# PEER routing of a two-layer trunk: one comparison and one product per eight tokens for the one-hot tiles, and sub-key scores issued in turns

## The chip, the cores and the metric

The kernel runs on one core of one Trainium2 chip. The metric is the device time of one execution in microseconds; each kernel is run several times and the median counts. The engines have short names in the profile: PE is the matrix engine (PEld its weight loads), DVE the vector engine, ACT the scalar engine, POOL the general-purpose engine, SP the engine whose queue issues most of the transfers.

## The reference

The reference is one inference step of a two-layer trunk over 128 context tokens and 512 latent tokens of width 1024. Each layer is a token mixer followed by a PEER expert mixer. Both are normalised and modulated; only the expert mixer matters here:

```python
q = (xc @ wq).reshape(P_BLOCK, P_HEADS, 2, P_DKEY // 2)
s = jnp.einsum('chpd,hpkd->chpk', q, sub_keys)
sv, si = lax.top_k(s, P_TOPK)                       # 16 of 128 per head and half
cand = sv[:, :, 0, :, None] + sv[:, :, 1, None, :]  # 16 x 16 candidates
fs, fi = lax.top_k(cand, P_TOPK)                    # 16 experts per head
eidx = jnp.take_along_axis(cidx, fi, axis=-1)       # cidx = i * 128 + j
g = jax.nn.softmax(fs, axis=-1)
act = jax.nn.gelu(jnp.einsum('cd,chkd->chk', xc, u[eidx]))
return jnp.einsum('chk,chkd->cd', g * act, v[eidx])
```

There are 8 heads, two halves of 64 numbers each, 128 sub-keys per half and 16384 experts, each named by a pair (i, j).

## The kernel before

The program runs mixer 0, PEER 0, mixer 1, PEER 1. A PEER layer has two phases.

In the routing phase (502 to 985 us in layer 0, the same again about 2005 us later in layer 1) the tokens come in five tiles of 128: tile 0 is the context, tiles 1 to 4 are latent. `scores` multiplies each tile's queries with the sub-keys: sixteen products of 64 rows, eight on the lower 64 rows of PE (row tile 0) and eight on the upper (row tile 1), in groups of four into one PSUM buffer, which ACT copies to SBUF. There are two such buffers (tag `sp`), shared with the transposes of `to_hk`. `topk` does the two-stage selection on DVE: sixteen rounds over the sub-keys, eight rounds (one for each head, five operations each) over the candidates `cand`, then the softmax weights `g` (the difference on DVE, Exp on ACT, the sum `gs` on DVE), and one-hot selections `eq` of 2048 elements that give the expert's `i` and `j` (tile `ij`).

For latent tokens the kernel does not gather experts. It computes all products S = u . h with PE (one S tile is 128 experts by 512 tokens, 24 matmuls: `h2h` and `h2l` are the tokens in two parts, `uh` and `ul` the expert rows in two parts, `uh` cast by ACT and `ul` made by DVE at L220; `ge` is the Gelu of S on ACT) and a matrix G of the weights, 128 by 128 per token. 72 of the 128 S tiles are computed in the routing phase, between its steps (`S_ahead`). G of a token is the product of two one-hot matrices. `to_hk` transposes i, j and g on PE, ACT copies them to `iT`, `jT` and, via `g32`, DVE makes the two halves `gh` and `gl` of g. For each group of eight tokens `build` makes on DVE the one-hot tile `oj` of j, the one-hot tile `oi` of i, and its products with `gh` and `gl` (both called `o`), 1024 half-precision elements per partition each. `place` multiplies on PE, sixteen small matmuls per group into two PSUM buffers called `G` (four in rotation), which ACT copies out into `stg`. Sixteen groups belong to a tile; those of tile tt are built and placed while the top-k of the next tile runs, and the last sixteen in a tail after tile 4. Groups 0 to 63 count through a layer.

The program is written in the order of the loops, but the framework's list scheduler decides the order of instructions on each engine in the routing phase. Each engine then works through its row strictly in order. The phase that follows, in which the expert outputs are computed, keeps the written order.

Of the kernel before, what the change touches and what calls it, by code (L numbers as in the profile page):

```python
# [13 lines left out]
F32 = mybir.dt.float32  # L14
F32R = mybir.dt.float32r
F16 = mybir.dt.float16
# [4 lines left out]
OP = mybir.AluOpType  # L21
# [4 lines left out]
P = 128  # L26
# [3 lines left out]
TS = 512  # L30
# [22 lines left out]
def _trunk(ctx, tc, nc, I, O, n_phases):  # L53
# [12 lines left out]
    ident = const("ident", [P, P])  # L66
# [1049 lines left out]
    def peer(l, last_layer):  # L1116
        with ExitStack() as s:
# [45 lines left out]
            with ExitStack() as s2:  # L1163
                qp = s2.enter_context(tc.tile_pool(reuse_waits="tile", name=f"pq{l}", bufs=1))
                sub = qp.tile([P, 8, P], F32, name=f"sub{l}")
                nc.sync.dma_start(sub, I["subT"][l])
                qT = qp.tile([P, 8, T], F32, name=f"qT{l}")
                with ExitStack() as s3:
                    wp = s3.enter_context(tc.tile_pool(reuse_waits="tile", name=f"pw{l}", bufs=2))
                    tp = s3.enter_context(tc.tile_pool(reuse_waits="tile", name=f"pt{l}", bufs=2))  # L1170
# [24 lines left out]
                    for n in range(NC):  # L1195
                        wh, wl, raw = ws.pop(n) if n in ws else wload(wp, I["pwq"][l, n], P, "w")
                        ps = ppn.tile([P, 2, 512], F32, name=f"pqs{l}_{n}", tag="b2")
                        for c in range(NC):
                            for k, (a, b) in enumerate(((wh, h2h), (wl, h2h), (wh, h2l))):
                                nc.tensor.matmul(ps[:, 0, :], a[:, c], b[:, c], start=(c == 0 and k == 0),  # L1200
                                                 stop=(c == NC - 1 and k == 2))
                        for c in range(NC):
                            nc.tensor.matmul(ps[:, 1, :TP], raw[:, c], ph32[:, c], start=(c == 0),
                                             stop=(c == NC - 1))
# [3 lines left out]
                    for x in range(2):  # L1208
                        ps = ppn.tile([P, 2, 512], F32, name=f"phT{l}_{x}", tag="b2")
# [4 lines left out]
                cp = s2.enter_context(tc.tile_pool(reuse_waits="tile", name=f"pc{l}", bufs=1))  # L1214
                tp = s2.enter_context(tc.tile_pool(reuse_waits="tile", name=f"pk{l}", bufs=2))
                ohp = s2.enter_context(tc.tile_pool(reuse_waits="tile", name=f"poh{l}", bufs=2))
                pk = s2.enter_context(tc.tile_pool(reuse_waits="tile", name=f"ppk{l}", bufs=2, space=PSUM))
                iota16 = cp.tile([P, 16, 8], F16, name=f"iota16{l}")
                nc.sync.dma_start(iota16, I["iota"])
                iota2 = cp.tile([P, P, 2], F16, name=f"iota2{l}")  # L1220
                nc.sync.dma_start(iota2, I["iota2"])
                iT = cp.tile([P, TS], F16, name=f"iT{l}")
                jT = cp.tile([P, TS], F16, name=f"jT{l}")
                gh = cp.tile([P, TS], F16, name=f"gh{l}")
                gl = cp.tile([P, TS], F16, name=f"gl{l}")

                def scores(tt):
                    nm = f"{l}_{tt}"
                    sc_ = tp.tile([P, 16, P], F32, name=f"sc{nm}", tag="sc", bufs=1)
                    for q4 in range(4):  # L1230
                        p, h0 = q4 % 2, (q4 // 2) * 4
                        rr = slice(p * 64, (p + 1) * 64)
                        ps = pk.tile([P, 4, P], F32, name=f"scp{nm}_{q4}", tag="sp")
                        for r in range(4):
                            nc.tensor.matmul(ps[:, r], qT[rr, h0 + r, tt * P:(tt + 1) * P], sub[rr, h0 + r],
                                             start=True, stop=True)
                        nc.scalar.copy(sc_[:, h0 * 2 + p:h0 * 2 + 8:2], ps)
                    return sc_

                def topk(tt, sc_, step):  # L1240
                    nm = f"{l}_{tt}"
                    sv = tp.tile([P, 16, 16], F32, name=f"sv{nm}", tag="sv")
                    si = tp.tile([P, 16, 16], U32, name=f"si{nm}", tag="si")
                    for r in range(16):
# [7 lines left out]
                    sif = tp.tile([P, 2, 16, 8], F16, name=f"sif{nm}", tag="sif")  # L1252
                    nc.vector.tensor_copy(sif.rearrange("p q a h -> p h q a"),
                                          si.rearrange("p (h q) a -> p h q a", q=2))
                    cand = tp.tile([P, 8, 112], F32, name=f"cand{nm}", tag="cand", bufs=1)
                    svh = sv.rearrange("p (h q) a -> p h q a", q=2)
                    nc.vector.tensor_tensor(
                        cand[:, :, 0:64].rearrange("p h (a b) -> p h a b", b=16),
# [20 lines left out]
                    gs = tp.tile([P, 8], F32, name=f"gs{nm}", tag="gs")  # L1279
# [20 lines left out]
                    def hk(t):  # L1300
# [3 lines left out]
                                            op=OP.subtract)  # L1304

                    ij = tp.tile([P, 2, P], F32, name=f"ij{nm}", tag="ij", bufs=1)
                    for q in range(2):
                        step(25 + 3 * q)
                        eq = tp.tile([P, 16, 16, 8], F16, name=f"eq{nm}_{q}", tag="eq", bufs=1)
                        nc.vector.tensor_tensor(eq, abk[:, q].unsqueeze(1).to_broadcast([P, 16, 16, 8]),  # L1310
                                                iota16.unsqueeze(2).to_broadcast([P, 16, 16, 8]),
                                                op=OP.is_equal)
                        nc.vector.tensor_tensor(eq, eq, sif[:, q].unsqueeze(2).to_broadcast([P, 16, 16, 8]),
                                                op=OP.mult)
                        for w in (8, 4, 2):
                            nc.vector.tensor_tensor(eq[:, :w], eq[:, :w], eq[:, w:2 * w], op=OP.add)
                        nc.vector.tensor_tensor(ij[:, q].rearrange("p (k h) -> p k h", h=8), eq[:, 0], eq[:, 1],
                                                op=OP.add)
# [1 line left out]
                    return gk, ij  # L1320

                def to_hk(tt, g, ij):
                    ts = slice((tt - 1) * P, tt * P)
                    ps = pk.tile([P, 4, P], F32, name=f"hk{l}_{tt}", tag="sp")
                    nc.tensor.transpose(ps[:, 0], ij[:, 0], ident)
                    nc.tensor.transpose(ps[:, 1], ij[:, 1], ident)
                    nc.tensor.transpose(ps[:, 2], g, ident)
                    nc.scalar.copy(iT[:, ts], ps[:, 0])
                    nc.scalar.copy(jT[:, ts], ps[:, 1])
                    g32 = tp.tile([P, P], F32, name=f"g32{l}_{tt}", tag="g32")  # L1330
                    nc.scalar.activation(g32, ps[:, 2], AF.Copy, scale=GSC)
                    nc.vector.tensor_copy(gh[:, ts], g32)
                    nc.vector.tensor_tensor(gl[:, ts], g32, gh[:, ts], op=OP.subtract)

                stg = [None]

                def build(grp):

                    ts = slice(grp * 8, (grp + 1) * 8)

                    def bc(t):
                        return (t[:, ts].rearrange("p (b t) -> p b t", t=2).unsqueeze(2)
                                .to_broadcast([P, 4, P, 2]))
                    io = iota2.unsqueeze(1).to_broadcast([P, 4, P, 2])
                    oj = ohp.tile([P, 4, P, 2], F16, name=f"oj{l}_{grp}", tag="oj")
                    oi = ohp.tile([P, 4, P, 2], F16, name=f"oi{l}_{grp}", tag="oi", bufs=1)
                    o1 = ohp.tile([P, 4, P, 2], F16, name=f"o1{l}_{grp}", tag="o1")
                    o2 = ohp.tile([P, 4, P, 2], F16, name=f"o2{l}_{grp}", tag="o2")
                    nc.vector.tensor_tensor(oj, bc(jT), io, op=OP.is_equal)  # L1349
                    nc.vector.tensor_tensor(oi, bc(iT), io, op=OP.is_equal)  # L1350
                    nc.vector.tensor_tensor(o1, oi, bc(gh), op=OP.mult)
                    nc.vector.tensor_tensor(o2, oi, bc(gl), op=OP.mult)
                    return oj, o1, o2

                def place(grp, oj, o1, o2):
                    if grp % 4 == 0:
                        stg[0] = ohp.tile([P, P, 32], F32, name=f"stg{l}_{grp}", tag="stg")
                    for q in range(2):
                        ps = pk.tile([P, 4, P], F32, name=f"G{l}_{grp}_{q}", tag="G", bufs=4)
                        for r in range(4):  # L1360
                            t = q * 4 + r
                            b, h = t // 2, t % 2
                            nc.tensor.matmul(ps[:, r], oj[:, b, :, h], o1[:, b, :, h], start=True, stop=False)
                            nc.tensor.matmul(ps[:, r], oj[:, b, :, h], o2[:, b, :, h], start=False, stop=True)  # L1364
                        t0 = (grp % 4) * 8 + q * 4
                        nc.scalar.activation(stg[0][:, :, t0:t0 + 4].rearrange("p i t -> p t i"), ps,  # L1366
                                             AF.Copy, scale=1.0 / GSC)
                    if grp % 4 == 3:
                        for a, b in ((0, NI),) if grp < 63 else ((0, 8), (8, NI)):
                            nc.sync.dma_start(Gd[grp // 4, :, a:b], stg[0][:, a:b])  # L1370
# [18 lines left out]
                for tt in range(NT):  # L1389
# [6 lines left out]
                    sc_ = scores(tt)  # L1396
# [3 lines left out]
                    g, ij = topk(tt, sc_, step)  # L1400
# [21 lines left out]
            with ExitStack() as s2:  # L1422
# [156 lines left out]
                with tc.manual_schedule():  # L1579
# [5 lines left out]
                    for y in range(NMAIN[0], CH, 2):  # L1585
                        r = rp.tile([P, 2, TS], F32, name=f"gr{l}_{y}", tag="row")
# [5 lines left out]
                    for cc in range(NB):  # L1592
                        nm = NMAIN[cc]
                        todo = None
                        ges = {}
                        for x in range(nm):
                            i = cc * CH + x
                            ps = S_mm(i, us.pop(i))
# [55 lines left out]
                        for dt in range(NC):  # L1654
                            n = cc * NC + dt
                            ps = out_mm(n, order)
# [151 lines left out]
```

## Time and profile before

| | us |
|---|---|
| Median of 3 runs | 4017.03 (4014.59 to 4021.36) |
| Profiled execution | 4011.71 |
| Its span in the trace | 4009.9 |
| PE busy | 3900.3 (97%) |
| DVE busy | 2955.4 (74%) |
| ACT busy | 1554.4 (39%) |
| POOL busy | 726.7 (18%) |

The profiled execution was 5.3 us below the median of the runs; outside its span lie 1.8 us. Times below count from the span's start. A row of a timeline gives start, duration, engine, line, operation, written tile `<-` read tiles and, in brackets, the idle time ahead of the instruction and what ended it. An engine starts an operation before the one ahead has wholly ended, so the step from start to start is shorter than the duration when nothing is waited for.

### The profile page before, as it was taken

To read this page: it belongs to the slowest core of one execution; us is meant where nothing else is said; L and a number is where in the kernel's file an instruction comes from. 1 tells how busy PE (TensorE), PEld (TensorE's weight loads), DVE (VectorE), ACT (ScalarE), POOL (GpSimd) and SP (SyncE) were. 2 spreads that over 40 slices of the span, in tenths; PEclk is the share of its full clock that TensorE was granted. 3 is DMA by queue.
4 is the path that set the end of the run, shared out by engine and by line. 5 is a ranking of instruction groups with operands and counts; after the bars stand their busy time and mean duration, and the time that the engine had idled before them with its cause. 6 is when DMAs were issued, how large, how long until landed. Compare 5 with 4: busy or idle time off the path is not lost.

```text
span 4009.9 us, 57042 instructions
## 1 busy us (share of the span) xinstructions
PE 3900.3 (97%) x21578; PEld 3242.2 (81%) x21578; DVE 2955.4 (74%) x6091; ACT 1554.4 (39%) x2320; POOL 726.7 (18%) x687
## 2 busy tenths in 40 slices
PE   7989999999999999999999999999999999999998
PEld 5958887888888888888889778888887888888887
DVE  5265389996778778787775663899967777777875
ACT  3344235566332322323343552355663323223231
POOL 0000000000334333243100110000003343333432
PEclk9989999999999999999999999999999999999999
DMA  5144134556888888888552012345568888888884
GB/s 181 55 169 143 54 126 179 200 195 248 295 278 296 294 283 305 272 294 299 193 183 87 17 38 70 127 178 201 195 248 296 280 295 293 285 303 272 297 301 166
DMA packets 363929, 850.80 MB, mean 212 GB/s; under 512 B 27858, under 2 KB 172164, under 8 KB 356868
## 3 DMA queue, kind: packets, MB, share of 16 engines
q1 hardware_dynamic: 289012, 576.04, 41.3%
q0 software_dynamic: 74640, 271.10, 19.5%
q8 instruction: 170, 2.79, 0.3%
q14 instruction: 107, 0.88, 0.1%
HBM read 738.12 MB, written 108.92 MB: 211 GB/s over the span
## 4 chain that ended last, share of the span: by engine, by line
PE 70%; DVE 13%; issue 8%; DMA 4%; ACT 3%; POOL 2%; SPq 0%; POOLq 0%; DVEq 0%; ACTq 0%
PE O L1528 9%; PE O L1532 9%; PE O L1529 9%; PE S L1141 8%; PE S L1142 7%; PE S L1144 7%; PE ow L246 4%; PE pqs L1200 2%; PE et L246 2%; DVE ul L220 2%; PE ef L435 1%; PE ewops L335 1%; PE owops L335 1%; POOL gu L1435 1%; PE CS L979 1%
## 5 line engine op out<-in xcount | busy, mean ns | idle before, releaser
L1141 PE MATMUL S<-h2h,uh 128*128 128x512 f32 x2048 | 811.8, 397 | 9.7 <-ACT ge L1149 5.5
L1528 PE MATMUL O<-Wh,vh 128*128 128x512 f32 x2048 | 798.3, 390 | 7.4 <-ACT Wh L1491 5.0
L1142 PE MATMUL S<-h2l,uh 128*128 128x512 f32 x2048 | 799.6, 391 | 0.0
L1529 PE MATMUL O<-Wh,vl 128*128 128x512 f32 x2048 | 797.3, 389 | 0.0
L1532 PE MATMUL O<-Wl,vh 128*128 128x512 f32 x2048 | 781.7, 389 | 0.0
L1144 PE MATMUL S<-h2h,ul 128*128 128x512 f32 x2048 | 589.4, 389 | 0.0
L219 ACT CAST vh<-v_raw 128x1024 fp32r<-128x1024 f32 x256 | 269.7, 1053 | 804.4 <-PE O L1532 754.4
L1435 POOL DMA_INDIRECT gv<-in_pv_dram,eidx x256 | 356.5, 1393 | 795.2 <-DVE acc L1451 771.1
L1141 PEld LDWEIGHTS S<-h2h,uh 128*128 128x128 f32 x2048 | 385.6, 188 | 94.9 <-ACT uh L219 7.8
L1528 PEld LDWEIGHTS O<-Wh,vh 128*128 128x128 f32 x2048 | 384.7, 188 | 90.2 <-ACT Wh L1491 7.2
L1532 PEld LDWEIGHTS O<-Wl,vh 128*128 128x128 f32 x2048 | 384.8, 188 | 80.4
L1144 PEld LDWEIGHTS S<-h2h,ul 128*128 128x128 f32 x2048 | 384.4, 188 | 80.0
L220 DVE TENSOR_TENSOR ul<-u_raw,uh 128x1024 fp32r<-128x1024 f32 x256 | 312.2, 1220 | 185.7 <-ACT uh L219 141.1
L1529 PEld LDWEIGHTS O<-Wh,vl 128*128 128x128 f32 x2048 | 384.8, 188 | 79.3
L1142 PEld LDWEIGHTS S<-h2l,uh 128*128 128x128 f32 x2048 | 386.0, 188 | 76.9
L1435 POOL DMA_INDIRECT gu<-in_pu_dram,eidx x256 | 321.5, 1256 | 520.3 <-DVE dots L1442 369.3
L219 ACT CAST uh<-u_raw 128x1024 fp32r<-128x1024 f32 x256 | 269.1, 1051 | 338.3 <-PE S L1142 312.4
L220 DVE TENSOR_TENSOR vl<-v_raw,vh 128x1024 fp32r<-128x1024 f32 x256 | 312.4, 1220 | 113.3 <-ACT vh L219 110.1
L1451 DVE SCALAR_TENSOR_TENSOR acc<-gv,dots,acc 128x1024 f32<-128x1024 f32 x256 | 327.7, 1280 | 44.8 <-DMA gv<-in_pv_dram,eidx 42.5
L1442 DVE CUSTOM_DVE_ANT_0 gu<-gu,h2p 128x1024 f32<-128x1024 f32 x256 | 311.3, 1219 | 48.4 <-DMA gu<-in_pu_dram,eidx 47.0
L1366 ACT ACTIVATE stg<-G 128x512 f32<-128x512 f32 x256 | 261.0, 1161 | 0.7 <-PE G L1364 0.7
L1429 POOL MEMSET acc<- 128x1024 f32 x2 | 1.9, 958 | 1338.9 <-DVE oj L1349 760.1
(402 smaller groups left out, 5909.4 us busy)
## 6 DMA issues: line engine op xcount, KB each, us to landing
u_raw<-in_uT_dram SPq DMA_DIRECT2D x256, 512.0 KB
v_raw<-in_vR_dram SPq DMA_DIRECT2D x256, 512.0 KB
gt<-Gd SPq DMA_DIRECT2D x64, 1024.0 KB
Gd<-stg SPq DMA_DIRECT2D x30, 2048.0 KB
adaw<-in_adaw_dram SPq DMA_DIRECT2D x80, 512.0 KB
Sd<-ge SPq DMA_DIRECT2D x144, 256.0 KB
gr<-Sd SPq DMA_DIRECT2D x134, 256.0 KB
w_raw<-in_ow_dram SPq DMA_DIRECT2D x12, 1024.0 KB
```

The lines of the kernel that those rows point to most:

```text
L219: nc.scalar.copy(hi, raw)
L220: nc.vector.tensor_tensor(lo, raw, hi.bitcast(F32), op=OP.subtract)
L1141: nc.tensor.matmul(ps, hi[:, c], h2h[:, c], start=(c == 0), stop=False)
L1142: nc.tensor.matmul(ps, hi[:, c], h2l[:, c], start=False, stop=False)
L1144: nc.tensor.matmul(ps, lo[:, c - 5], h2h[:, c - 5], start=False, stop=(c == NC + 5 - 1))
L1366: nc.scalar.activation(stg[0][:, :, t0:t0 + 4].rearrange("p i t -> p t i"), ps, AF.Copy, scale=1.0 / GSC)
L1435: nc.gpsimd.indirect_dma_start(out=r[:], out_offset=None, in_=I[table], in_offset=bass.IndirectOffsetOnAxis(ap=eidx2[:, k:k + 1], axis=0))
L1442: nc.vector.tensor_tensor_reduce(r, r, h2p, 1.0, 0.0, OP.mult, OP.add, dots[:, k:k + 1])
L1451: nc.vector.scalar_tensor_tensor(acc, r, dots[:, k:k + 1], acc, op0=OP.mult, op1=OP.add)
L1528: nc.tensor.matmul(ps, hi[:, order[y]], Wh, start=(y == 0), stop=False)
L1529: nc.tensor.matmul(ps, lo[:, order[y]], Wh, start=False, stop=False)
L1532: nc.tensor.matmul(ps, hi[:, x], Ws[n // NC * CH + x][1], start=False, stop=(y == CH + lag - 1))
```

## The change

`iT` and `jT` become one tile `jiT`, `gh` and `gl` one tile `ghl`, each laid out by groups of eight tokens. `build` makes both one-hot tiles with one comparison of 2048 elements (`oo`) and both gated tiles with one product of 2048 elements (`og`), in which the one-hot half of i is read twice. `oo` and `og` have two buffers each; before, `oj` and the two `o` had two and `oi` one. `cand` shares a buffer with `eq`. In `scores` two PSUM buffers are opened at once and the matmuls are written in turns on the two row tiles, the copies behind them.

```diff
-                    for q4 in range(4):
-                        p, h0 = q4 % 2, (q4 // 2) * 4
-                        rr = slice(p * 64, (p + 1) * 64)
-                        ps = pk.tile([P, 4, P], F32, name=f"scp{nm}_{q4}", tag="sp")
+                    for h0 in (0, 4):
+                        pss = [pk.tile([P, 4, P], F32, name=f"scp{nm}_{h0}_{p}", tag="sp") for p in range(2)]
+
                         for r in range(4):
-                            nc.tensor.matmul(ps[:, r], qT[rr, h0 + r, tt * P:(tt + 1) * P], sub[rr, h0 + r],
-                                             start=True, stop=True)
-                        nc.scalar.copy(sc_[:, h0 * 2 + p:h0 * 2 + 8:2], ps)
+                            for p, ps in enumerate(pss):
+                                rr = slice(p * 64, (p + 1) * 64)
+                                nc.tensor.matmul(ps[:, r], qT[rr, h0 + r, tt * P:(tt + 1) * P], sub[rr, h0 + r],
+                                                 start=True, stop=True)
+                        for p, ps in enumerate(pss):
+                            nc.scalar.copy(sc_[:, h0 * 2 + p:h0 * 2 + 8:2], ps)
...
-                    cand = tp.tile([P, 8, 112], F32, name=f"cand{nm}", tag="cand", bufs=1)
+                    cand = tp.tile([P, 8, 112], F32, name=f"cand{nm}", tag="eq", bufs=1)
...
-                    nc.scalar.copy(iT[:, ts], ps[:, 0])
-                    nc.scalar.copy(jT[:, ts], ps[:, 1])
+                    for q in range(2):
+                        nc.scalar.copy(jiT[:, gs, q], by8(ps[:, q]))
...
-                    io = iota2.unsqueeze(1).to_broadcast([P, 4, P, 2])
-                    oj = ohp.tile([P, 4, P, 2], F16, name=f"oj{l}_{grp}", tag="oj")
-                    oi = ohp.tile([P, 4, P, 2], F16, name=f"oi{l}_{grp}", tag="oi", bufs=1)
-                    o1 = ohp.tile([P, 4, P, 2], F16, name=f"o1{l}_{grp}", tag="o1")
-                    o2 = ohp.tile([P, 4, P, 2], F16, name=f"o2{l}_{grp}", tag="o2")
-                    nc.vector.tensor_tensor(oj, bc(jT), io, op=OP.is_equal)
-                    nc.vector.tensor_tensor(oi, bc(iT), io, op=OP.is_equal)
-                    nc.vector.tensor_tensor(o1, oi, bc(gh), op=OP.mult)
-                    nc.vector.tensor_tensor(o2, oi, bc(gl), op=OP.mult)
-                    return oj, o1, o2
+                    oo = ohp.tile([P, 8, P, 2], F16, name=f"oo{l}_{grp}", tag="oo")
+                    og = ohp.tile([P, 8, P, 2], F16, name=f"og{l}_{grp}", tag="og")
+                    nc.vector.tensor_tensor(oo, bc(jiT), iota2.unsqueeze(1).to_broadcast([P, 8, P, 2]),
+                                            op=OP.is_equal)
+                    nc.vector.tensor_tensor(
+                        og.rearrange("p (q b) v t -> p q b v t", q=2),
+                        oo[:, 4:].unsqueeze(1).to_broadcast([P, 2, 4, P, 2]),
+                        bc(ghl).rearrange("p (q b) v t -> p q b v t", q=2), op=OP.mult)
+                    return oo, og
...
-                            nc.tensor.matmul(ps[:, r], oj[:, b, :, h], o1[:, b, :, h], start=True, stop=False)
-                            nc.tensor.matmul(ps[:, r], oj[:, b, :, h], o2[:, b, :, h], start=False, stop=True)
+                            nc.tensor.matmul(ps[:, r], oo[:, b, :, h], og[:, b, :, h], start=True, stop=False)
+                            nc.tensor.matmul(ps[:, r], oo[:, b, :, h], og[:, 4 + b, :, h], start=False, stop=True)
```

The scheduler answers with another order on DVE, PE and ACT. The first place is DVE's row in tile 3 of layer 0 around the build of group 24 (`fs`, `po` and `c_3_5` are the top-k of the candidates, the last number of `c` being the head; lines from L1236 on move by one or two between the versions). Before:

```order
L220 TENSOR_TENSOR ul_77_7464<-u_77_raw,uh_77_7465 128x1024
L1349 TENSOR_TENSOR oj_24_7388<-jT_4511,iota_4508 128x1024
L1351 TENSOR_TENSOR o_24_7390<-oi_24_7389,gh_4512 128x1024
L1352 TENSOR_TENSOR o_24_7391<-oi_24_7389,gl_4513 128x1024
L1272 MATCH_REPLACE c_3_5_7612<-fs_3_7427,cand_3_7424 128x112
L1350 TENSOR_TENSOR oi_25_7430<-iT_4510,iota_4508 128x1024
L1273 MAX fs_3_7427<-c_3_5_7612 128x8
```

The same place in the change:

```order
L1273 MATCH_REPLACE c_3_6_7563<-fs_3_7325,cand_3_7322 128x112
L1271 MAX fs_3_7325<-cand_3_7322 128x8
L1274 MAX fs_3_7325<-c_3_6_7563 128x8
L220 TENSOR_TENSOR ul_77_7358<-u_77_raw,uh_77_7359 128x1024
L1348 TENSOR_TENSOR oo_24_7290<-jiT_4510,iota_4508 128x2048
L1275 MAX_INDEX po_3_7326<-fs_3_7325,c_3_6_7563 128x8
L1350 TENSOR_TENSOR og_24_7291<-oo_24_7290,ghl_4511 128x2048
```

Before, head 5 is worked on behind the build of group 24; in the change the rounds of heads 5 and 6 stand ahead of it. The second place is a little later in the same row, around the build of group 25. Before, behind the softmax difference `g_3`:

```order
L1277 TENSOR_TENSOR g_3_7693<-fs_3_7427 128x128
L1288 TENSOR_SCALAR sh_3_7701<-po_3_7428 128x128
L1289 TENSOR_SCALAR sh_3_7701<-po_3_7428 128x128
L220 TENSOR_TENSOR ul_78_7538<-u_78_raw,uh_78_7539 128x1024
L1349 TENSOR_TENSOR oj_25_7429<-jT_4511,iota_4508 128x1024
L1351 TENSOR_TENSOR o_25_7431<-oi_25_7430,gh_4512 128x1024
L1352 TENSOR_TENSOR o_25_7432<-oi_25_7430,gl_4513 128x1024
L1349 TENSOR_TENSOR oj_26_7504<-jT_4511,iota_4508 128x1024
```

In the change (`fl`, `ab`, `abk` are small steps between the top-k and the one-hot selection `eq`):

```order
L1292 CAST fl_3_7586<-sh_3_7583 128x256
L1295 SCALAR_TENSOR_TENSOR ab_3_7589<-fl_3_7586 128x128
L1296 TENSOR_SCALAR fl_3_7586<-ab_3_7589 128x128
L1303 CAST abk_3_7593<-ab_3_7589 128x8x16
L1297 SCALAR_TENSOR_TENSOR fl_3_7586<-ab_3_7589,fl_3_7586 128x128
L1311 TENSOR_TENSOR eq_3_0_7656<-abk_3_7593,iota_4506 128x2048
L1281 TENSOR_REDUCE gs_3_7578<-g_3_7575 128x8
L220 TENSOR_TENSOR ul_78_7428<-u_78_raw,uh_78_7429 128x1024
L1348 TENSOR_TENSOR oo_25_7327<-jiT_4510,iota_4508 128x2048
L1348 TENSOR_TENSOR oo_26_7398<-jiT_4510,iota_4508 128x2048
L1350 TENSOR_TENSOR og_25_7328<-oo_25_7327,ghl_4511 128x2048
```

The steps from `fl` to `gs`, with a 2048-element `eq`, and the comparison of group 26 now stand ahead of `og_25`. On PE the order of S tiles and groups in tiles 2 to 4 is that of before. The third place is on PE in the tail, where group 50 meets S tile 115. Before:

```order
L1141 MATMUL S_115_9236<-h2h_4053,uh_115_9231 128x512
L1142 MATMUL S_115_9236<-h2l_4054,uh_115_9231 128x512
L1363 LDWEIGHTS oj_50_9174
L1363 MATMUL G_50_0_9210<-o_50_9176,oj_50_9174 128x128
L1363 LDWEIGHTS oj_50_9174
L1363 MATMUL G_50_1_9220<-o_50_9176,oj_50_9174 128x128
L1141 MATMUL S_115_9236<-h2h_4053,uh_115_9231 128x512
L1142 MATMUL S_115_9236<-h2l_4054,uh_115_9231 128x512
L1364 LDWEIGHTS oj_50_9174
L1364 MATMUL G_50_0_9210<-o_50_9177,oj_50_9174 128x128
```

In the change, where these rows come after twelve matmuls of `S_115`:

```order
L1141 MATMUL S_115_9026<-h2h_4053,uh_115_9021 128x512
L1142 MATMUL S_115_9026<-h2l_4054,uh_115_9021 128x512
L1364 LDWEIGHTS oo_50_8972
L1364 MATMUL G_50_0_9000<-og_50_8973,oo_50_8972 128x128
L1365 LDWEIGHTS oo_50_8972
L1365 MATMUL G_50_0_9000<-og_50_8973,oo_50_8972 128x128
```

Group 50 is no longer begun with two matmuls inside the S tile; its sixteen stand together in the middle of it. Groups 57 and 62 move in the same way.

## Rows read from the trace of the kernel before

**Rows 1.** The page: busy time of the engines, and the chain that ended last by engine.
```profile
PE 3900.3 (97%) x21578; PEld 3242.2 (81%) x21578; DVE 2955.4 (74%) x6091; ACT 1554.4 (39%) x2320; POOL 726.7 (18%) x687
...
PE 70%; DVE 13%; issue 8%; DMA 4%; ACT 3%; POOL 2%; SPq 0%; POOLq 0%; DVEq 0%; ACTq 0%
```

**Rows 2.** Windows, layer 0: length, busy PE, PEld, DVE, ACT, POOL; clock, DMA share, GB/s.
```profile
616.00:710.00 94.00, 93.64 (x590) 77.36 (x591) 93.66 (x300) 54.71 (x65) 0.00 (x0) 1.00 0.52 185
710.00:808.00 98.00, 96.09 (x624) 79.21 (x623) 95.48 (x301) 59.37 (x70) 0.00 (x0) 1.00 0.54 200
808.00:907.00 99.00, 97.07 (x628) 80.08 (x627) 94.98 (x300) 59.54 (x70) 0.00 (x0) 1.00 0.55 197
907.00:985.00 78.00, 76.49 (x548) 63.13 (x547) 53.63 (x78) 54.47 (x62) 0.96 (x1) 1.00 0.70 255
```

**Rows 3.** Waits of PE, 500 to 990 us: us in total, times, longest.
```profile
PE G L1363 <- ACT stg L1366: 3.1, 6, 1.1
PE S L1141 <- ACT ge L1149: 3.0, 2, 1.8
...
PE G L1364 <- DVE o L1352: 1.0, 3, 0.4
PE hk L1326 <- DVE ij L1317: 0.8, 1, 0.8
```

**Rows 4.** Groups of instructions on DVE: count, busy us and mean ns, idle before.
```profile
L1350 DVE TENSOR_TENSOR oi<-iT,iota 128x1024 f16<-128x1024 f16 x128 | 88.4, 690 | 8.6 <-ACT iT L1328 7.9
...
L1313 DVE TENSOR_TENSOR eq<-eq,sif 128x2048 f16<-128x2048 f16 x20 | 24.9, 1246 | 0.4
```

**Rows 5.** Timeline of DVE in tile 2: a 2048-element product and what follows.
```profile
700.58 1.22 DVE L1313 TENSOR_TENSOR eq<-eq,sif 128x2048 f16<-128x2048 f16 x1
701.71 0.68 DVE L1350 TENSOR_TENSOR oi<-iT,iota 128x1024 f16<-128x1024 f16 x1
```

**Rows 6.** Timeline of DVE in tile 3.
```profile
713.80 0.69 DVE L1350 TENSOR_TENSOR oi<-iT,iota 128x1024 f16<-128x1024 f16 x1 [1.30 <-ACT iT L1328]
...
764.97 0.08 DVE L1272 MATCH_VALUE_LOAD c<-fs,cand 128x8 f32 x1
...
766.05 0.08 DVE L1272 MATCH_VALUE_LOAD c<-fs,cand 128x8 f32 x1
...
768.86 0.69 DVE L1351 TENSOR_TENSOR o<-oi,gh 128x1024 f16<-128x1024 f16 x1
769.46 0.69 DVE L1352 TENSOR_TENSOR o<-oi,gl 128x1024 f16<-128x1024 f16 x1
770.07 0.09 DVE L1272 MATCH_VALUE_LOAD c<-fs,cand 128x8 f32 x1
...
776.59 0.68 DVE L1352 TENSOR_TENSOR o<-oi,gl 128x1024 f16<-128x1024 f16 x1
```

**Rows 7.** Timeline of PE in tile 3, groups 24 and 25.
```profile
769.71 0.22 PE L1363 MATMUL G<-o,oj 128*128 128x128 f16 x1
770.21 0.22 PE L1364 MATMUL G<-o,oj 128*128 128x128 f16 x1 [0.28 <-DVE o L1352]
...
777.34 0.22 PE L1363 MATMUL G<-o,oj 128*128 128x128 f16 x1 [0.59 <-ACT stg L1366]
...
778.26 0.22 PE L1363 MATMUL G<-o,oj 128*128 128x128 f16 x1 [0.30 <-ACT stg L1366]
```

**Rows 8.** Timeline of ACT in tile 3, Exp of `g`.
```profile
774.09 0.31 ACT L1278 ACTIVATE g<-g 128x128 f32<-128x128 f32 x1 [4.12 <-DVE g L1277]
```

**Rows 9.** Timeline of PE in tile 2, group 9.
```profile
678.83 0.22 PE L1364 MATMUL G<-o,oj 128*128 128x128 f16 x1 [0.36 <-DVE o L1352]
```

**Rows 10.** Timeline of PE in the tail, group 50.
```profile
920.42 0.29 PE L1363 MATMUL G<-o,oj 128*128 128x128 f16 x2 [1.09 <-ACT stg L1366]
```

**Rows 11.** Scores: chain by time (start, us, what), and PE's timeline.
```profile
504.06 1.71 PE scp L1235 x16
...
712.38 1.16 PE L1235 MATMUL scp<-sub,qT 64*128 64x128 f32 x8
```

More of the change, by code (lines that the diff above doesn't have):

```diff
@@ L1221, in peer @@
                 nc.sync.dma_start(iota2, I["iota2"])
[L1222 to L1225, printed above, removed]
+                jiT = cp.tile([P, TS // 8, 2, 8], F16, name=f"jiT{l}")
+                ghl = cp.tile([P, TS // 8, 2, 8], F16, name=f"ghl{l}")
                 def scores(tt):
@@ L1322, in to_hk, with by8 @@
                 def to_hk(tt, g, ij):
-                    ts = slice((tt - 1) * P, tt * P)
+                    gs = slice((tt - 1) * 16, tt * 16)
+                    def by8(t):
+                        return t.rearrange("p (b t) -> p b t", t=8)
                     ps = pk.tile([P, 4, P], F32, name=f"hk{l}_{tt}", tag="sp")
-                    nc.tensor.transpose(ps[:, 0], ij[:, 0], ident)
-                    nc.tensor.transpose(ps[:, 1], ij[:, 1], ident)
+                    nc.tensor.transpose(ps[:, 0], ij[:, 1], ident)
@@ L1327, in to_hk @@
+                    nc.tensor.transpose(ps[:, 1], ij[:, 0], ident)
                     nc.tensor.transpose(ps[:, 2], g, ident)
-                    nc.scalar.copy(iT[:, ts], ps[:, 0])
-                    nc.scalar.copy(jT[:, ts], ps[:, 1])
+                    for q in range(2):
+                        nc.scalar.copy(jiT[:, gs, q], by8(ps[:, q]))
                     g32 = tp.tile([P, P], F32, name=f"g32{l}_{tt}", tag="g32")
                     nc.scalar.activation(g32, ps[:, 2], AF.Copy, scale=GSC)
-                    nc.vector.tensor_copy(gh[:, ts], g32)
@@ L1333, in to_hk @@
-                    nc.vector.tensor_tensor(gl[:, ts], g32, gh[:, ts], op=OP.subtract)
+                    nc.vector.tensor_copy(ghl[:, gs, 0], by8(g32))
+                    nc.vector.tensor_tensor(ghl[:, gs, 1], by8(g32), ghl[:, gs, 0], op=OP.subtract)
                 stg = [None]
                 def build(grp):
-                    ts = slice(grp * 8, (grp + 1) * 8)
                     def bc(t):
-                        return (t[:, ts].rearrange("p (b t) -> p b t", t=2).unsqueeze(2)
-                                .to_broadcast([P, 4, P, 2]))
@@ L1351, in build @@
-                    nc.vector.tensor_tensor(o1, oi, bc(gh), op=OP.mult)
-                    nc.vector.tensor_tensor(o2, oi, bc(gl), op=OP.mult)
-                    return oj, o1, o2
-                def place(grp, oj, o1, o2):
+                        return (t[:, grp].rearrange("p q (b t) -> p (q b) t", t=2).unsqueeze(2)
+                                .to_broadcast([P, 8, P, 2]))
+                    oo = ohp.tile([P, 8, P, 2], F16, name=f"oo{l}_{grp}", tag="oo")
+                    og = ohp.tile([P, 8, P, 2], F16, name=f"og{l}_{grp}", tag="og")
@@ new lines, in build, with place @@
+                    nc.vector.tensor_tensor(oo, bc(jiT), iota2.unsqueeze(1).to_broadcast([P, 8, P, 2]),
[5 more added lines that the diff above has]
+                    return oo, og
+                def place(grp, oo, og):
```

## The prediction

> **What bounds the kernel now.** The page comes first: PE is busy for 97% of the span, and 70% of the chain that ended last is PE, 13% DVE [rows 1]. DVE can therefore matter only where it holds PE up. The busy time by stage shows where: while tiles 2 to 4 are routed, DVE is as full as PE (93.66 against 93.64 of 94 us, 95.48 against 96.09 of 98); in the tail after tile 4 DVE has room (53.63 of 78) [rows 2]. Both parts of the change lie in these routing stages, two per program, and the built order outside them is row for row that of before. The idle time of PE in one layer's four stages from 616 to 985 us is at most 6 us, so the change can win little; what it can lose is open. The list of waits of PE names its pieces for layer 0: 3.1 us for ACT's `stg` copies, 3.0 for two `ge`, 1.0 for the gated tile, 0.8 for `ij` [rows 3]. Layer 1 has the same rows within 0.5 us.
>
> **The price of a build.** A 1024-element half-precision comparison takes 690 ns, a 2048-element product with an operand repeated along one axis 1246 [rows 4]. What counts on a full engine is the step to the next start: two 1024 products take 768.86 to 770.07, so 0.605 each, and a 2048 product with independent work behind it 1.13 (700.58 to 701.71) [rows 5, 6]. A build goes from 4 x 0.605 = 2.42 to 2 x 1.13 = 2.26; over all rows of the kind it is nearer 0.14 than 0.16, and I take 0.15 saved. Where a product stands right behind its own comparison I bound the step by the full 1246 ns, so a build costs 2.26 to 2.5; in the order one operation stands between nearly everywhere, so 2.26. Sixteen builds give DVE 2.4 us per tile. That is worth something only if the order leaves it in front of what PE waits for.
>
> **Where PE waits for a build.** I compared the end of each `o` product with the start of its group's matmuls on PE. Of the 48 groups placed in tiles 2 to 4 and at their borders, 42 have 3.4 us or more to spare; groups 9, 24, 25, 40 and 41 have none, and group 8 has 0.17. The reason is the order of PE: groups 7 and 8 (23 and 24, 39 and 40) stand together with no S tile between them. So the question is when the gated tile of 8, 9, 24, 25, 40 and 41 is done.
>
> Tile 3, counted from the first build, which starts when ACT has copied the indices (713.80 [rows 6]; one copy of about 0.2 us later after the change, since one tile now holds both rows). Ahead of `og_24` stand nine more top-k operations than ahead of the last `o_24`: heads 5 and 6 are worked on earlier, as the order rows show. A head's five take 764.97 to 766.05, so 0.216 each [rows 6], 1.95 in all. Nine cheaper builds give 1.35 back. `og_24` ends 1.95 - 1.35 + 0.2 = 0.8 us later than 770.07, and PE's second matmul of the group, which in before waited 0.28 and ran at 770.21 [rows 7], comes about 0.75 later.
> Ahead of `og_25` stand `oo_26` (1.13), the first 2048 comparison `eq` (1.24) and seven small operations on the candidates (at 0.2 to 0.22, 1.5); ten builds give 1.5 back. It ends 1.13 + 1.24 + 1.5 - 1.5 + 0.2 = 2.6 later than 776.59 + 0.60 = 777.19, so at 779.8. In before PE starts this group at 777.34 after 0.59 of waiting, and waits 0.30 more at 778.26, both for `stg` copies [rows 7]; these queue on ACT behind the Exp of `g`, which waited 4.12 for DVE [rows 8]. In the change `g` stands before that extra work and comes 1.6 us earlier, so the copies are on time and that wait is gone; PE instead waits for `og_25` until 779.85. The place loses 779.85 - 777.34 - 0.30 = 2.2 us: a wait of 0.9 for ACT turns into about 2.5 for DVE. Tile 4 has the same rows at groups 40 and 41, 99 us on.
>
> Tile 2, counted the same way: ten more top-k operations ahead of `og_8` (+2.15 - 1.35 = 0.8 late), `oo_10` and nine small operations ahead of `og_9` (1.13 + 1.9 - 1.5 = 1.5 late). Group 9 waited 0.36 in before and ran on at 678.83 [rows 9]; it runs 1.4 later. What follows in each tile has 3.4 us or more to spare, so nothing is late next; the delay stays, since PE has no idle time to absorb it.
> Cost: two layers x (1.4 + 2.2 + 2.2) = 11.6 us.
>
> **What is won.** In the tail group 50 is begun two matmuls at a time inside an S tile, and PE waits 1.09 us there [rows 10]; although the copy is named, the group's first product ends just then. Groups 57 and 62 do the same with 0.2 each. In the change each stands whole behind 12 matmuls of the S tile. `og_50` is then ready about 0.4 after PE arrives; 0.7 + 0.4 are won, and three pairs of switches between S and G (0.08 each way) make 0.5: 1.6 per layer, 3.2 in all. In tile 0 of layer 0 a `uh` cast moves from between Exp and the next `ge` to ahead of them; of the 1.2 us that PE waits there (3.0 less the longest, 1.8 [rows 3]), 0.95 go. In layer 1 the cast moves behind both instead, and the S tile that needs it waits: nothing. Tile 1's 1.8 goes too, but DVE has no gap there and sets the transposes at its end: 0 in layer 0, at most 0.6 in layer 1; I take 0.3.
>
> **The scores in turns.** In the built program the turns remain in tiles 0 and 1 alone; in tiles 2, 3 and 4 the order on PE is four matmuls on one row tile, then four on the other, as before. Sixteen instructions that run over the border between the row tiles take 1.71 us, eight on one alone 1.16 [rows 11]: they do overlap where they meet, but there is little room. The second half of a block waits for ACT's copies out of two PSUM buffers in both versions, and behind tiles 0 and 1 DVE's top-k sets the pace; worth 0.
> The Trainium skill, page "TensorEngine Tiling (Array Packing)", Overview, Theoretical Speedup, allows up to 2x for operands of 64 rows; if it held for all ten blocks it would be the fourth rival below. The same page, Performance Considerations, PSUM Bottleneck, says that tiling speeds TensorE and not the emptying of PSUM, and that the copy may become the limit; the waits for the copies between the halves agree.
>
> **Sum.** 11.6 - 3.2 - 0.95 - 0.3 = +7.1 us. The profiled execution took 4011.71, so 4018.8 profiled; the median of the runs lies 5.3 above it, so about 4024.
>
> **Rivals.**
> Second, faster: DVE is not late. This needs the two 2048 operations to cost 2.0 us together, not 2.26, so that ten builds give back 2.6 more; then the 0.9 for ACT goes in tiles 3 and 4 as well, and 3.2 + 0.95 + 0.3 + 4 x 0.9 = 8 are won: 4009. For it speaks that `g` and `ij` come earlier in the order; against it the 1.13 step.
> Third, clearly slower: each 2048 operation holds DVE its full 1.24, as where the next one depends on it. Then a build costs 2.5, 0.24 more than assumed, and by the tenth build `og` is 2.2 later, at three places in each of two layers: 6 x 2 = 12 more, 4036. It decides from a step of about 1.2 up.
> Fourth: the turns halve the scores in every tile. A block of 32 instructions at 1.71 per 16 is 3.4; ten blocks x 1.7 = 17 won: 4024 - 17 = 4007. Against it: the order of tiles 2 to 4.
> Fifth: the product with its repeated operand runs at the rate of single elements, about 2.3 us instead of 1.13 (twice 1.13). 128 x 1.15 = 147 on a DVE that is full in most of it: 4160. Against it: the 2048-element product of [rows 4], whose operand is repeated too, takes 1246 ns.
>
> **Chances.** First case 0.66 (its own range 4016 to 4031, since each of the six late ends is uncertain by 1 us), second 0.18, third 0.11, fourth 0.04, fifth 0.01. A measurement of this kernel can tell about 0.2%, 8 us, from no change. The first case lies on that bound from below: 0.28 of its chance beyond it, 0.36 within, 0.02 ahead. The second gives 0.13 faster and 0.05 within; the third and fifth are slower; the fourth faster 0.03, within 0.01. Together faster 0.18, same 0.42, slower 0.40. The range reaches from the second case's start to the third: 4007 to 4036.
>
> **What would show it.** Right: `G` waits for `og` of 1 to 2.6 us at groups 9, 25 and 41 of each layer, no wait for `stg` there, group 50's wait 0.4, the steps of `oo` and `og` 1.13. Wrong: `og_25` done before 778, steps of 1.2 or more, PE waits at other groups, or scores in turns in tiles 2 to 4.

## The result, and the profile after

| | before | after |
|---|---|---|
| Median, us | 4017.7 (5 runs) | 4040.2 (4033.15 to 4042.01, 5 runs) |
| Ratio | | 1.0051, 95% interval 1.0041 to 1.0062 |
| Profiled execution, us | 4011.71 | 4033.15 |
| DVE busy, us | 2955.4 | 2937.3 |

The change makes the kernel about 20 us slower (22.5 between the medians, 20.5 by the ratio), although DVE has 18 us less to do. The prediction had 4024, with 4007 to 4036 as its range. The page after, same lines as [rows 1] (busy time, and the chain that ended last by engine):

```profile
PE 3905.1 (97%) x21578; PEld 3245.0 (80%) x21578; DVE 2937.3 (73%) x5835; ACT 1553.1 (39%) x2320; POOL 726.4 (18%) x687
...
PE 79%; DVE 12%; DMA 3%; ACT 3%; issue 2%; POOL 1%; SPq 0%; DVEq 0%; POOLq 0%; ACTq 0%
```

The groups of the two new operations on DVE, to hold beside [rows 4] (count, busy us, mean ns, idle time before them):

```profile
L1348 DVE TENSOR_TENSOR oo<-jiT,iota 128x2048 f16<-128x2048 f16 x128 | 154.1, 1218 | 14.8 <-ACT jiT L1333 8.9 <-PE G L1365 5.8
...
L1350 DVE TENSOR_TENSOR og<-oo,ghl 128x2048 f16<-128x2048 f16 x128 | 153.5, 1215 | 0.8
```

So the operations cost what the 2048-element rows of before cost; nothing is slow in them. The time is lost on PE. Its waits in layer 0, the list of [rows 3] (us in total, times, longest):

```profile
PE G L1364 <- DVE og L1350: 8.4, 7, 2.3
PE hk L1329 <- DVE ij L1318: 3.8, 1, 3.8
PE scp L1235 <- ACT g L1335: 1.2, 2, 0.6
PE S L1141 <- ACT ge L1149: 1.0, 1, 1.0
```

The waits for `stg` and one of the two for `ge` are gone; in their place are 8.4 us for the gated tile and one wait of 3.8 us for `ij` ahead of the first transposes. The windows of [rows 2] again, with two more (length, busy PE, PEld, DVE, ACT, POOL; clock, DMA share, GB/s). The line ahead of them is before, the six behind it are the change:

```profile
614.00:630.00 16.00, 15.23 (x96) 12.61 (x95) 15.89 (x56) 8.02 (x13) 0.00 (x0) 1.00 0.30 98
...
614.00:630.00 16.00, 15.18 (x76) 12.96 (x77) 12.09 (x47) 4.89 (x10) 0.00 (x0) 0.68 0.26 81
616.00:710.00 94.00, 92.53 (x564) 76.38 (x564) 88.59 (x265) 52.10 (x60) 0.00 (x0) 0.95 0.47 171
710.00:808.00 98.00, 93.89 (x606) 77.45 (x604) 92.39 (x268) 57.80 (x68) 0.00 (x0) 1.00 0.53 192
808.00:907.00 99.00, 94.89 (x609) 78.16 (x608) 89.75 (x266) 57.35 (x68) 0.00 (x0) 0.98 0.52 188
907.00:985.00 78.00, 77.58 (x571) 64.61 (x569) 54.94 (x49) 56.21 (x64) 0.96 (x1) 1.00 0.67 255
886.00:889.00 3.00, 3.00 (x16) 2.61 (x14) 3.00 (x6) 2.12 (x3) 0.00 (x0) 0.50 1.02 434
```

The column to read is the granted clock. Before it was 1.00 in all these stages of layer 0 [rows 2]; now it is 0.68 from 614 to 630 us and 0.50, the lower of its two levels (1.2 of 2.4 GHz), from 886 to 889. PE's timeline ahead of the first of these stretches shows what it did before (start, duration, operation, idle time):

```profile
614.82 0.30 PE L1329 MATMUL hk<-ident,ij 128*128 128x128 f32 x1 [3.75 <-DVE ij L1318]
...
615.27 5.60 PE L1235 MATMUL scp<-sub,qT 64*128 64x128 f32 x32
620.79 0.79 PE L1141 MATMUL S<-h2h,uh 128*128 128x512 f32 x1
621.39 0.63 PE L1142 MATMUL S<-h2l,uh 128*128 128x512 f32 x1
621.81 0.63 PE L1141 MATMUL S<-h2h,uh 128*128 128x512 f32 x1
```

PE is idle for 3.75 us. Then a block of scores takes 5.60 us, where one with the same order of row tiles takes 3.92 at the full clock (run `e4_more_S_in_tile1`, below), and matmuls of an S tile follow each other every 0.43 us and not every 0.23. The Trainium skill, page "TensorE: Matmul & The Clock Gate", Part 1, HAM oscillation, says that idle stretches of PE bring the lower clock back and that each return is paid again; the row agrees.

The same matmul compared in the two traces tells where the lateness arises (start after minus start before, us, each counted from its span's start; of a group, the first product that needs the second half of g):

| | layer 0 | layer 1 |
|---|---|---|
| start of the routing (first product of the scores) | -0.2 | +7.5 |
| behind the scores of tile 0 | -0.9 | +6.7 |
| group 0 (behind the first transposes) | +3.4 | +10.4 |
| group 10 (tile 2) | +4.5 | +11.5 |
| group 26 (tile 3) | +6.6 | +15.1 |
| group 42 (tile 4) | +10.2 | +18.7 |
| group 63 (tail) | +8.9 | +17.4 |

From the start of the routing to group 63 that is 9.1 us in layer 0 and 10.0 in layer 1. Outside the routing, where the program is the same, the traces drift apart too, by 1.5 us one way between the layers and 4 the other way behind the second.

How much of it is the clock can be estimated from the same traces. In the two routing phases the stretches at 0.50 add up to 27 us in the change and to 3 before; at half the clock that is about 12 of the 19 us. The rest is waiting, less what the turns and the tail save.

### The profile page after: what moved, and what is told of

Same layout as the page of the kernel before. It is cut to its first block, busy times and chain, and to the rows that moved or that the text cites. A ratio compares the mean times of both kernels' runs of the same rounds, so it can differ in the third digit from the quotient of the medians.

```text
span 4031.4 us, 56824 instructions
## 1 busy us (share of the span) xinstructions
PE 3905.1 (97%) x21578; PEld 3245.0 (80%) x21578; DVE 2937.3 (73%) x5835; ACT 1553.1 (39%) x2320; POOL 726.4 (18%) x687
## 4 chain that ended last, share of the span: by engine, by line
PE 79%; DVE 12%; DMA 3%; ACT 3%; issue 2%; POOL 1%; SPq 0%; DVEq 0%; POOLq 0%; ACTq 0%
PE O L1533 11%; PE O L1529 11%; PE O L1530 11%; PE S L1141 8%; PE S L1142 8%; PE S L1144 8%; PE ow L246 4%; PE pqs L1200 2%; PE et L246 2%; PE ef L435 1%; PE ewops L335 1%; DVE oo L1348 1%; PE owops L335 1%; DVE ul L220 1%; PE CS L979 1%
```

## The experiments

Theory A: the loss has two parts. First, PE now reaches the transposes of tile 1 earlier than DVE has the indices, stands idle in one piece and runs at the lower clock behind it. Second, the order on DVE makes the gated tiles of groups 8, 9, 24, 25, 40 and 41 late. Theory B: the wider operations hold DVE longer, and the order has nothing to do with it. All ratios are to the kernel before, with 95% intervals; the changed kernel itself is at 1.0051.

**The two parts of the change alone.** `e1_turns_only` is the kernel before with the new `scores`:

```diff
-                    for q4 in range(4):
...
+                    for h0 in (0, 4):
+                        pss = [pk.tile([P, 4, P], F32, name=f"scp{nm}_{h0}_{p}", tag="sp") for p in range(2)]
```

> Scores in turns alone; builds, gated tiles and their order as before. Theory A (the loss has two parts: PE reaches the first transposes of tile 1 earlier than DVE has the indices, stands idle for 3.8 us, and then runs at a lower granted clock; and the order on DVE puts the gated tiles late in tiles 2 to 4): only the first part is left. The built order of ACT in tiles 0 and 1 is that of the changed kernel. PE waits 3.8 us for ij in each layer, the granted clock falls to 0.5 for some us behind it, +3.5 us in layer 0 and +1.5 in layer 1: about 4022 to 4023, the waits for the gated tile as before (0.4 and below). Theory B (the whole loss comes from the builds: the wider operations hold DVE longer): no loss here, 4017 or a little below. Theory C (turns save PE time in the scores): 4010 or below.

Measured: 4020.96, ratio 1.0011 (1.0002 to 1.0020). Its waits of PE in layer 0, and the window behind the first transposes:

```profile
PE hk L1328 <- DVE ij L1319: 3.6, 1, 3.6
PE G L1365 <- ACT stg L1368: 3.1, 6, 1.1
...
614.00:630.00 16.00, 12.45 (x54) 10.43 (x53) 15.66 (x49) 4.00 (x9) 0.00 (x0) 0.68 0.38 123
```

The long wait and the drop of the clock come with the turns, without any change to the builds; the `stg` waits are those of before. Theory C falls: the turns make the kernel slower.

`e2_builds_only` is the changed kernel with the old `scores`.

> One comparison and one product per build; scores as before. Theory A: only the second part is left. ACT's order in tiles 0 and 1 is that of before, PE waits 1.8 us for ge and 0.8 for ij as before, no clock drop there; waits for og of 0.4 to 2.3 us at groups 8, 9, 24, 25, 40 and 41 as in the changed kernel, 1.2 + 2.0 to 3.7 + 2.5 to 3.7 us per layer, less 1.3 in the tail: +11 to 15 in all, 4029 to 4033. Theory B: the whole loss, 4040. Theory C (builds are free and the turns cost everything): 4017.

Measured: 4033.93, ratio 1.0040 (1.0026 to 1.0054), 0.9 us above what was expected. The same two views:

```profile
PE G L1362 <- DVE og L1348: 8.1, 7, 2.3
PE S L1141 <- ACT ge L1149: 3.0, 2, 1.8
...
PE hk L1327 <- DVE ij L1316: 1.0, 1, 1.0
...
614.00:630.00 16.00, 14.98 (x94) 12.39 (x93) 15.69 (x53) 8.31 (x13) 0.00 (x0) 1.00 0.34 108
```

Here the clock stays at 1.00 at the transposes, and PE waits 8.1 us for `og`. The two ratios add up to the whole, each with an interval of about 0.001 either way: 0.0011 + 0.0040 = 0.0051.

**Is it the idle time or the clock?** `e3_filler` puts matmuls into the hole:

```diff
+                    if tt == 1:
+                        for c in range(12):
+                            nc.tensor.matmul(ps, h2h[:, c % NC, :P], h2h[:, c % NC], start=True, stop=True)
                     nc.tensor.transpose(ps[:, 0], ij[:, 1], ident)
```

> The changed kernel with twelve more matmuls of 512 columns per layer, into the PSUM tile that the transposes of tile 1 then overwrite; the output is the same. They stand on PE right ahead of these transposes, where PE waits 3.75 us, and take 2.7 us. Theory A: the wait shrinks to about 1 us, the granted clock stays at 1.0 behind it, the scores of tile 2 take 3.5 instead of 5.6 us, and each layer is 4.5 us shorter although PE does more work: about 4031. Theory D (the time is lost by waiting for DVE alone, the clock is a by-product that costs nothing here): 4040, no change.

Measured: 4030.43, ratio 1.0032 (1.0020 to 1.0045). PE's timeline at the same place, and the window:

```profile
615.22 2.88 PE L1331 MATMUL hk<-h2h 128*128 128x512 f32 x12
619.06 0.33 PE L1332 MATMUL hk<-ident,ij 128*128 128x128 f32 x1 [0.96 <-DVE ij L1318]
...
621.39 0.50 PE L1141 MATMUL S<-h2h,uh 128*128 128x512 f32 x1
...
614.00:630.00 16.00, 15.04 (x97) 12.03 (x96) 15.86 (x49) 6.88 (x12) 0.00 (x0) 1.00 0.43 134
```

PE does 2.9 us more work per layer, the transposes still wait for DVE, and the program is 10 us shorter than the changed one. In layer 0 the transposes start 112.6 us after the first product of the scores, in the changed kernel 112.8; group 0 follows 4.9 us sooner. Theory D falls: waiting for DVE is not what costs this time, the clock behind the wait is. (The scheduler also sets the scores of tile 2 in two parts among the S matmuls in this kernel; they take PE about 0.7 us less, which is part of the 4.9.)

The granted clock of whole executions agrees: its mean is 0.9830 over the five of the changed kernel, 0.9853 over the six of this one and 0.9861 to 0.9867 over those of before. A thousandth of the span is 4 us, so by this estimate 9 of the 10 us are clock.

**Filling the hole with work that has to be done.** `e4_more_S_in_tile1` moves one S tile into it:

```diff
-                    share = 0.12 if tt < 2 else 0.195
+                    share = (0.12, 0.134, 0.19, 0.19, 0.19)[tt]
```

> The changed kernel with the share of tile 1 in the S tiles raised from 0.12 to 0.134 and of tiles 2 to 4 lowered to 0.19: one more S tile (5.4 us of PE) stands ahead of the first transposes, one fewer in the later tiles, the total is the same. Theory A: the wait for ij (3.75 us) goes, no clock drop, 4.5 to 6 us less per layer, and the waits for og move to other groups, since groups without an S tile between are now 6/7, 18/19, 25/26; 4026 to 4034. Theory D: 3.75 us less for each layer at most, 4033 or above. Theory B: the builds still hold DVE, 4036 to 4040.

Measured: 4013.38, ratio 0.9989 (0.9980 to 0.9998): 27 us less than the changed kernel, and 13 below the range that was expected. The waits of PE in layer 0, the end of tile 1, and the window:

```profile
PE G L1364 <- DVE og L1350: 6.3, 6, 1.9
...
618.64 0.27 PE L1329 MATMUL hk<-ident,ij 128*128 128x128 f32 x1
...
619.06 3.92 PE L1235 MATMUL scp<-sub,qT 64*128 64x128 f32 x32
...
614.00:630.00 16.00, 16.00 (x100) 13.61 (x99) 15.10 (x49) 6.89 (x12) 0.00 (x0) 1.00 0.46 142
```

The transposes wait for nothing, the clock stays up there, and 6.3 us for `og` are left, none of them longer than 1.9. What the expectation lacked is the clock behind these waits too: in this profile it falls behind none of them, in that of the changed kernel behind three of four waits of 2.3 us. The mean clock is 0.9864 against 0.9830, an estimated 14 of the 27 us; most of the rest is the 7.5 us for `ij` in the two layers and 3 less for `og`. `f1_before_more_S` makes the same edit in the kernel before:

> The kernel before with one S tile moved from the later tiles to tile 1 (shares 0.134 and 0.19). It tells whether the 4013 of the same move in the changed kernel belongs to the move alone. Theory A: before has no clock drop to lose, only waits of 0.8 and 1.8 us in tile 1, so it gains 0 to 5 us: 4012 to 4017. Theory F (the move is worth as much in any version, 27 us): 3990.

Measured: 4017.58, ratio 0.9999 (0.9991 to 1.0008). The kernel before has no clock to win back at the transposes (its mean over the executions is 0.9863 with the move and 0.9866 without) and gains nothing; theory F falls.

**Is it the order that makes og late?** In before, `oi` of the next group stood behind the products of the current one, because it had a buffer of its own. `f2_third_oo` gives `oo` a third buffer, and the operations stay the same:

```diff
-                    oo = ohp.tile([P, 8, P, 2], F16, name=f"oo{l}_{grp}", tag="oo")
+                    oo = ohp.tile([P, 8, P, 2], F16, name=f"oo{l}_{grp}", tag="oo", bufs=3)
```

> The changed kernel with a third buffer for the one-hot tile oo (og keeps two). The scheduler then sets the comparison of the next group behind the product of the current one, as oi stood in before: by the order, og of groups 24 and 25 has 1.4 and 3.1 us less work ahead of it on DVE than in the changed kernel, and the same at 8, 9, 40 and 41. Theory A (the order on DVE makes og late): the waits for og fall to 0.4 us or less, no clock drop in tiles 3 and 4; what is left is the 3.8 us wait for ij and the drop behind it, as in the run with the turns alone: about 4019 to 4022. Theory B (the wider operations hold DVE): the waits for og stay, 4038 to 4040.

Measured: 4020.17, ratio 1.0013 (1.0005 to 1.0022). First DVE in tile 3 of the changed kernel, then in this one; `og` of group 24 and what stands ahead of group 25:

```profile
774.15 1.20 DVE L1350 TENSOR_TENSOR og<-oo,ghl 128x2048 f16<-128x2048 f16 x1
775.28 0.08 DVE L1272 MATCH_VALUE_LOAD po<-fs,cand 128x8 f32 x1
...
778.33 1.23 DVE L1311 TENSOR_TENSOR eq<-abk,iota 128x2048 f16<-128x2048 f16 x1
...
780.80 2.36 DVE L1348 TENSOR_TENSOR oo<-jiT,iota 128x2048 f16<-128x2048 f16 x2
783.07 2.36 DVE L1350 TENSOR_TENSOR og<-oo,ghl 128x2048 f16<-128x2048 f16 x2
```

```profile
768.83 1.21 DVE L220 TENSOR_TENSOR ul<-u_raw,uh 128x1024 fp32r<-128x1024 f32 x1
769.95 1.22 DVE L1350 TENSOR_TENSOR og<-oo,ghl 128x2048 f16<-128x2048 f16 x1
771.09 1.22 DVE L1348 TENSOR_TENSOR oo<-jiT,iota 128x2048 f16<-128x2048 f16 x1
772.22 0.09 DVE L1275 MATCH_VALUE_LOAD po<-fs,c 128x8 f32 x1
```

With two buffers the comparison of group 25 comes after the end of the top-k and after `eq`, and two comparisons stand ahead of one product; with three it runs right behind the product of group 24, as `oi` did. The waits of PE in layer 0 of this kernel:

```profile
PE hk L1329 <- DVE ij L1318: 3.8, 1, 3.8
PE G L1364 <- DVE og L1350: 1.3, 3, 0.7
PE G L1364 <- ACT stg L1367: 1.3, 4, 0.3
```

The 8.4 us for `og` fall to 1.3, all of it in the tail, and the ratio is that of the turns alone. Theory B falls: operations of the same width, in another order, lose nothing. With the old scores as well, `g2_third_oo_old_scores`:

> One comparison and one product per build, a third buffer for oo, and the scores as before. Theory A: both parts of the loss are gone, no clock drop anywhere in the routing; what the builds save on DVE is worth the small waits for o and stg: 4012 to 4017. Theory B: 4033 as with the builds alone.

Measured: 4012.52, ratio 0.9995 (0.9986 to 1.0003): the loss is gone, and the merged builds are worth about what can be measured, or less. That the clock would fall nowhere in the routing did not come true: in the profile it is 0.50 for some 3 us in tile 4 of layer 0, behind a wait of 0.6 us of the scores, and in layer 1 behind a wait of 1.8 for `ge`.

**A version ahead of both.** `g1_third_oo_more_S` has the third buffer and the moved S tile.

> The changed kernel with a third buffer for oo and the S tile moved to tile 1. Theory A: neither the late og nor the clock drop is left, scores in turns and cheaper builds are worth a few us: 4003 to 4011, ahead of both kernels. Theory B: og still late, 4013 as without the third buffer.

Measured: 4008.45, ratio 0.9978 (0.9969 to 0.9987). Its waits of PE in layer 0, and a wait in the scores of tile 4 with the stretch behind it:

```profile
PE G L1364 <- DVE og L1350: 1.3, 4, 0.7
PE scp L1235 <- ACT g L1335: 1.2, 2, 0.6
PE S L1141 <- ACT ge L1149: 0.9, 1, 0.9
...
815.23 3.83 PE L1235 MATMUL scp<-sub,qT 64*128 64x128 f32 x24 [0.61 <-ACT g L1335]
...
817.20:823.90 6.70, 6.70 (x44) 6.19 (x45) 5.57 (x19) 4.77 (x6) 0.00 (x0) 0.50 0.18 79
```

The late `og` is gone, but the second half of the expectation, no clock drop, is not met: behind a wait of 0.6 us that every version has, the clock is at 0.50 for almost 7 us here and again in layer 1 (2725 to 2732 us).

`g3_third_oo_more_S_old_scores` takes the turns out of it again.

> The best version so far (third oo buffer, one S tile moved to tile 1) with the scores as before: it tells what the turns themselves are worth once nothing idles behind them. From the traces: with the turns PE reached the first transposes 3.3 to 3.8 us earlier in layer 0 (1 from the order of the uh cast, 0.7 from the scores of tile 1, 2.1 from the order of ge), 3.7 in layer 1 less 0.8 given back. If PE's time counts there now, 4008 plus 5 to 6: 4013 to 4015. If DVE still sets the transposes, 4008 to 4010.

Measured: 4008.57, ratio 0.9982 (0.9973 to 0.9991), the same: with the move in place the turns bring nothing on balance. The reason that was expected, DVE setting the transposes, is not it, since PE waits for `ij` in neither profile. The turns do save PE waits (3.4 us in all in layer 0 against 5.7), but the profile without them has no stretch at 0.50 in the routing, and the mean clock over the eleven executions of each is 0.9851 with the turns and 0.9864 without, an estimated 5 us. So what the turns save is about what the clock takes back; why it falls more often with them was not settled.

## Why the prediction was wrong

**The late gated tiles: right in place and cause.** The prediction put the waits at groups 8, 9, 24, 25, 40 and 41 and explained them by the top-k operations, `eq` and the next comparison that stand ahead of `og`. In the trace PE waits 1.06 us at group 24 and 2.32 at group 25, where it had said that group 24 comes 0.75 later and that about 2.5 us are waited for 25:

```profile
775.41 0.23 PE L1364 MATMUL G<-og,oo 128*128 128x128 f16 x1 [1.06 <-DVE og L1350]
...
784.35 0.23 PE L1364 MATMUL G<-og,oo 128*128 128x128 f16 x1 [2.32 <-DVE og L1350]
```

The step of a 2048-element operation, 774.15 to 775.28, is the 1.13 of the sum. Tile 2 cost 1.1 to 1.2 us per layer where 1.4 was said, tile 3 of layer 0 2.0 where 2.2 was said, the tail gave back 1.3 where 1.6 was said.

**A step that failed: "What follows in each tile has 3.4 us or more to spare, so nothing is late next; the delay stays".** No later build was late, but the sum priced a wait at its length and put the clock behind it at nothing. Behind group 41 of layer 0 PE runs at 0.50 of its clock (the window from 886 to 889), and the tile loses 3.6 us, not 2.2; the same behind groups 25 and 41 of layer 1, 3.6 each. The wait at group 41, and the clock behind the two in layer 1:

```profile
885.40 0.23 PE L1364 MATMUL G<-og,oo 128*128 128x128 f16 x1 [2.32 <-DVE og L1350]
...
2797.20:2800.40 3.20, 3.20 (x11) 2.56 (x9) 3.20 (x6) 1.80 (x2) 0.00 (x0) 0.50 0.99 425
2899.60:2902.80 3.20, 3.20 (x14) 2.68 (x12) 3.20 (x6) 2.02 (x3) 0.00 (x0) 0.50 1.01 431
```

These three places add 4.3 us to the sum.

**The step that failed most: "Tile 1's 1.8 goes too, but DVE has no gap there and sets the transposes at its end: 0 in layer 0".** That DVE sets the transposes was right, and in layer 0 DVE came 1.2 us earlier there. But the time that PE saved did not vanish. Ahead of the transposes of layer 0 PE stood 4.0 us earlier than in before: 0.2 from ahead of the routing, 0.7 from the scores of tile 0, 0.3 from tile 0's waits, 0.7 from the scores of tile 1 and 2.1 at the `ge`. The turns of the scores, which the prediction put at 0, are in this sum twice, with 0.7 us of PE for each block. Less DVE's 1.2, all of it joined the old wait for `ij` of 0.8 [rows 3] into one of 3.75. In layer 0 of before there were two short waits, 1.8 and 0.8, with two S tiles between them, and the clock stayed at 1.00. After the long one it fell.

From the start of the routing to group 0 the change lost 3.5 us in layer 0 and 2.9 in layer 1, where 0.95 and 0.3 of gain were forecast. `e3_filler` shows that most of this is the clock's doing. The term was mis-sized by 7.7 us; the forecast 7.1, this and the 4.3 above make the 19 us of the table. Layer 1 lost less, in part because before had paid there already: in its layer 1 the clock did fall, behind the wait of 1.8 for `ge` alone,

```profile
2610.00:2612.50 2.50, 2.50 (x8) 1.91 (x7) 2.43 (x4) 0.00 (x0) 0.00 (x0) 0.50 0.80 311
```

and the S tile that runs through this stretch is 5.6 us late in the change at its start and 3.8 behind it.

**Two small terms.** In tile 0 of layer 0 the forecast 0.95 was 0.3: the Exp still waits for DVE and the `ge` behind it still comes 1.0 late. In layer 1 the moved cast was put at nothing; there PE waits 1.5 us for `uh` and 0.5 for `ul` in tile 0, where it had waited 0.7 for `ge`, and the tile lost 1.5.

**The rivals.** The third, 4036 by operations that hold DVE their full 1.24 us, was nearest in time and has the wrong mechanism: the step is 1.13. The fourth had something right: in the two tiles where the turns survived the scheduler, the first sixteen instructions of a block take 1.16 us, what eight on one row tile took in before [rows 11]; the second sixteen take 1.49:

```profile
564.54 1.16 PE L1235 MATMUL scp<-sub,qT 64*128 64x128 f32 x16
...
566.53 1.49 PE L1235 MATMUL scp<-sub,qT 64*128 64x128 f32 x16
```

Against eight on one row tile the first half meets the factor of up to 2 that the Trainium skill gives ("TensorEngine Tiling (Array Packing)", Overview, Theoretical Speedup). Against the 1.71 of sixteen in the old order it is less, and a block saves PE 0.7 us, not 1.7. Joined to the wait for `ij`, this saving made the kernel slower.

## What to carry to other kernels

Work taken off an engine that then waits for another is not worth zero: it can join short waits into a long one, behind which PE's clock was lower in each profile here, so ask not only how much an engine waits but in how many pieces, and put real work into the hole. When two buffered operations are merged, count the buffers that the pieces had: the piece with a buffer of its own was what could run ahead, and a list scheduler answers its loss with another order of everything around it. Where PE waits is decided at single places (here six of 64 groups), so cost a change by what stands ahead of those, not by the engine's busy time.

## What the runs showed of the hardware

In the routing phases of the eleven profiles (before, the change and the nine runs) each of the 24 stretches of PE at 0.50 of its clock began within 3 us of the end of a wait. Waits of the same length were not all followed by one:

| wait of PE, us | how many | clock at 0.50 within 3 us |
|---|---|---|
| 3.5 to 3.8 (`ij`) | 6 | 6 |
| 2.3 (`og`) | 12 | 8 |
| 1.8 to 2.1 (`ge`, `og`) | 12 | 3 |
| 0.9 to 1.6 | 50 | 0 |
| 0.5 to 0.8, other than the next | 39 | 0 |
| 0.6, in the middle of a block of scores | 44 | 7 |

So a longer wait made the lower clock more frequent, but its length does not decide alone: the 0.6 us in the scores were at times followed by it, the 50 waits of 0.9 to 1.6 never. In the profiled execution of the changed kernel PE waits 2.32 us at group 25 and again 2.32 at group 41 of layer 0; behind the first the granted clock stays at 1.00 (710 to 808 us), behind the second it is 0.50 for some 3 us. What decides was not settled. Sixteen score instructions on alternating row tiles in the time of eight on one (1.16 us) is the full factor of two; the second sixteen of the block took 1.49.
